# One transformer step on one core: small products of a bidirectional scan joined into longer bursts, the convolution moved ahead of the scan

## The chip, the cores and the metric

One core of one Trainium2 chip runs the whole step. The metric is the device time of one execution in microseconds (us); several runs are taken and their median is given. The engines are TensorE (PE, matrix products), VectorE (DVE), ScalarE (ACT), GpSimd (POOL) and SyncE (SP), which issues all the DMAs here. [...]

## The reference

The step is one trunk layer of width D = 1024 over T = 640 tokens (512 latent, 128 context), in fp32. After a modulated norm, one projection gives r, k, v (512 each), the input of a convolution branch (GLU) and two merge gates. Branch r is a bidirectional RWKV-7 scan over 8 heads of 64:

```python
def step(S, inp):
    rt, wt, kt, vt, at, bt = inp
    sa = jnp.einsum('bhvk,bhk->bhv', S, at)
    S = S * wt[:, :, None, :] + sa[..., None] * bt[:, :, None, :] + vt[..., None] * kt[:, :, None, :]
    return S, jnp.einsum('bhvk,bhk->bhv', S, rt)
```

It is followed by a norm over each head, a bonus term, a gate g and a 512 to 1024 projection. Branch c is GLU, a depthwise convolution of width 31, a norm, swish and a 512 to 1024 projection. The two are merged by sigmoid gates, projected by w_o and added to x; then come the MLP (1024 to 4096, squared ReLU, back to 1024), a residual and a final norm. The final scan states of the context are an output too.

## The kernel before, in words

**Dense products.** Every big fp32 product is split into high and low parts and made of three matmuls (high by high, low by high, high by low) for each of 8 slices of D, 128 x 320 at a time. Weights come by DMA as raw blocks `wr` (256 KB, `splitter`, L240) and are split by ACT (`wh`) and DVE (`wl`). One block of outputs has 48 such matmuls; I call a single one a dense matmul.

**The scan.** The 8 heads go in four pairs p = 0 to 3. For each pair: `prep` makes operands in the tile `ARGH`; `gram` (called by `solve`) makes the Gram products of all 20 chunks of 64 tokens (10 in each direction) in pieces of 32; `inverse` inverts the 64 x 64 triangles, by small DVE operations and three DVE transposes, then by PE products of 32 x 16 and 32 x 32; `build` makes the chunk matrices in five groups of two chunks per direction (matrices `ZB`, `L`, `RB`, `M`, start states `S`); `chain` runs the state through the chunks of a group, a few 64 x 64 products each time and an ACT copy between them; `post` does the norms and gate and writes `out`p to DRAM, from where it is read back into `ath` and split for branch r's projection.

**The order.** A planner at build time (`pick`, `more`, `plan`) keeps these steps as lanes with a rank (`URGENT`) and puts dense matmuls between their bursts; the result is an order written out by hand for PE, DVE and ACT, and each engine goes through its own list in order. The dense blocks come from the list `todo`: k, v, r of each pair, GLU blocks (at place `GLU_AT`), gates, and the side products of branch c (`"c" in ready_sides`) and branch r (`"r" in ready_sides`), which cannot start before their branch is done. Every matmul of these lanes has the line L195 (`mm`), every DVE, ACT and POOL instruction L108, so that pieces are told apart by their tiles.

**The convolution.** `conv_all` waits until the inverse of pair 3 is done and pair 2 is built; five tiles of 128 tokens (`conv_tile`) then run in the buffers `prod`, `Nb`, `Gf`, `Gt` and `E` of the scan, and leave their result split in `ARGH`.

After both branches come w_o, the MLP and the final norm; the change does not touch them.

## Time and profile before

| | us |
|---|---|
| median of 3 runs (lowest, highest) | 1330.57 (1325.54, 1337.10) |
| profiled execution, its own time | 1323.99 |
| its span, first to last instruction | 1322.2 |
| start, up to the first lora2 product | 0 to 56 |
| dense products with the scan's lanes among them | 56 to 677 |
| no dense product on PE | 674 to 729.3 |
| side products, w_o, MLP, end | 729.3 to 1322.2 |

The page's digit rows cut the span into 40 slices of 33 us. A row of a timeline has the start, the length and how many records of the same kind it holds; a matmul's row gives its length in the pipeline, so that the distance of two starts is the cost of one. A small fp32 product leaves two records. What stands in square brackets is how long the engine was idle before, and what ended that.

### The profile page before, as it was taken

How to read it: one execution, taken by the hardware profiler on the slowest of the kernel's cores; microseconds unless marked ns; L12 is line 12 of the kernel's file. 1: busy time of each engine (PE TensorE's matmuls, PEld its weight loads, DVE VectorE, ACT ScalarE, POOL GpSimd, SP SyncE). 2: the span in 40 equal slices, each digit the busy share in tenths (PEclk: the TensorE clock that was granted, in tenths of full speed). 3: DMA queues.
4: the chain of work that ended last, by engine and by line, in shares of the span. 5: the costliest groups of instructions: out<-in, count | busy, mean ns of one | idle time of the engine just before them, and what ended most of it. 6: DMA issues, size and time to landing. Idle time of an engine off the chain costs nothing.

```text
span 1322.2 us, 30685 instructions
## 1 busy us (share of the span) xinstructions
PE 1236.1 (93%) x13110; PEld 1094.7 (83%) x13110; DVE 654.0 (49%) x1342; ACT 505.3 (38%) x1149; POOL 31.4 (2%) x38
## 2 busy tenths in 40 slices
PE   8998899999999999999974899999999999999996
PEld 5776788777777878877741899999999999999996
DVE  5424575376465656245433566654443443443344
ACT  4445346436443643544212223344421331242130
POOL 0000000000000000100100000000000000000000
PEclk8989899999999999999976899989999999999998
DMA  9465433224222311231300683202222222222222
GB/s 371 144 207 171 149 117 122 78 67 150 80 78 81 124 43 58 87 92 54 100 26 8 209 286 122 74 32 78 73 75 81 72 72 81 80 71 74 81 73 80
DMA packets 77785, 136.14 MB, mean 103 GB/s; under 512 B 10768, under 2 KB 27824, under 8 KB 77648
## 3 DMA queue, kind: packets, MB, share of 16 engines
q1 hardware_dynamic: 77648, 134.17, 30.9%
q8 instruction: 103, 1.69, 0.5%
q14 instruction: 34, 0.28, 0.1%
HBM read 112.90 MB, written 21.23 MB: 101 GB/s over the span
## 4 chain that ended last, share of the span: by engine, by line
PE 86%; DVE 4%; ACT 3%; issue 3%; DMA 2%; SPq 0%; POOL 0%; POOLq 0%; DVEq 0%; ACTq 0%
PE ps_mm L195 45%; PE ps_b L195 21%; PE ps_t L195 12%; PE ps_a L195 6%; PE ps_ad L195 2%; DMA z<-tmp 1%; ACT Nb_w L108 1%; DMA par_t<-in_par 1%; DVE E_w L108 1%; DVE Gt_w L108 1%; ACT tmp L108 0%; DVE ARGH_t L108 0%; DMA g<-tmp 0%; DVE Gf_w L108 0%; ACT N_w L108 0%
## 5 line engine op out<-in xcount | busy, mean ns | idle before, releaser
L195 PE MATMUL ps_mm<-xh_t,wh_t 128*128 128x320 f32 x664 | 219.9, 331 | 1.2 <-ACT tmp L108 1.2
L195 PE MATMUL ps_mm<-xl_t,wh_t 128*128 128x320 f32 x664 | 219.8, 331 | 0.0
L195 PE MATMUL ps_mm<-xh_t,wl_t 128*128 128x320 f32 x664 | 217.1, 327 | 0.0
L108 ACT ACTIVATE wh_t<-wr_t 128x512 fp32r<-128x512 f32 x150 | 94.3, 629 | 141.0 <-PE ps_b L195 107.7
L108 DVE TENSOR_TENSOR wl_t<-wr_t,wh_t 128x512 fp32r<-128x512 f32 x150 | 102.8, 686 | 90.6 <-ACT wh_t L108 90.4
L195 PEld LDWEIGHTS ps_mm<-xh_t,wh_t 128*128 128x128 f32 x664 | 128.1, 193 | 19.8 <-issue 14.4
L195 PEld LDWEIGHTS ps_mm<-xl_t,wh_t 128*128 128x128 f32 x664 | 128.2, 193 | 14.6 <-issue 10.8
L195 PEld LDWEIGHTS ps_mm<-xh_t,wl_t 128*128 128x128 f32 x664 | 127.9, 193 | 12.4 <-issue 9.0
L195 PE MATMUL ps_mm<-ARGH_t,wh_t 128*128 128x320 f32 x284 | 77.8, 319 | 11.7 <-ACT wh_t L108 10.9
L108 ACT ACTIVATE tmp<-ps_mm 128x320 f32<-128x320 f32 x80 | 34.9, 436 | 96.7 <-PE ps_mm L195 90.8
L195 PE MATMUL ps_mm<-ARGH_t,wl_t 128*128 128x320 f32 x212 | 67.4, 318 | 0.0
L195 PEld LDWEIGHTS ps_mm<-ARGH_t,wh_t 128*128 128x128 f32 x284 | 53.1, 199 | 12.4 <-ACT wh_t L108 11.1
L108 ACT ACTIVATE mwh<-wr_t 128x512 fp32r<-128x512 f32 x49 | 31.1, 634 | 74.5 <-PE ps_b L195 69.9
L108 DVE TENSOR_TENSOR mwl<-wr_t,mwh 128x512 fp32r<-128x512 f32 x49 | 33.8, 690 | 38.6 <-ACT mwh L108 38.6
L108 DVE TENSOR_TENSOR tmp<-tmp 128x320 f32<-128x320 f32 x64 | 31.2, 489 | 42.7 <-ACT tmp L108 42.7
L108 DVE SCALAR_TENSOR_TENSOR ARGH_t<-ps_mm,mod_t,ARGH_t 128x320 f32<-128x320 f32 (+2 forms) x45 | 22.6, 511 | 59.4 <-PE ps_mm L195 59.4
L195 PE MATMUL ps_mm<-xl,wh_t 128*128 128x320 f32 x140 | 43.9, 314 | 0.0
L195 PE MATMUL ps_b<-ARGH_t,wl_t 128*128 128x320 f32 x140 | 43.2, 308 | 0.0
L195 PE MATMUL ps_b<-xl,wh_t 128*128 128x320 f32 x140 | 43.1, 308 | 0.0
L195 PE MATMUL ps_b<-ARGH_t,wh_t 128*128 128x320 f32 x140 | 42.6, 304 | 0.0
L195 PEld LDWEIGHTS ps_mm<-ARGH_t,wl_t 128*128 128x128 f32 x212 | 41.5, 196 | 0.4 <-DVE wl_t L108 0.4
L108 DVE SCALAR_TENSOR_TENSOR ARGH_t<-ps_b,mod_t,ARGH_t 128x128 f32<-128x128 f32 (+1 forms) x75 | 26.3, 390 | 20.0 <-PE ps_b L195 20.0
(372 smaller groups left out, 3027.6 us busy)
## 6 DMA issues: line engine op xcount, KB each, us to landing
wr_t<-in_w SPq DMA_DIRECT2D x225, 256.0 KB, 2.8
adl_w<-in_adal SPq DMA_DIRECT2D x64, 256.0 KB, 3.3
adar_s<-in_adaw SPq DMA_DIRECT2D x16, 512.0 KB, 8.4
ARGH_t<-in_x SPq DMA_DIRECT2D x8, 640.0 KB, 5.8
z<-tmp SPq DMA_DIRECT2D x32, 160.0 KB, 3.0
gate<-tmp SPq DMA_DIRECT2D x32, 160.0 KB, 1.8
tA_t<-z SPq DMA_DIRECT2D x8, 320.0 KB, 3.4
ath_t<-z SPq DMA_DIRECT2D x8, 320.0 KB, 3.4
```

Source lines behind the costliest of these rows:

```text
L108: return f(*args, **kw)
L195: PE.matmul(out=out, lhsT=lhsT, rhs=rhs, start=start, stop=stop, **kw)
```

## The change

1. Small products of one step are put into one run on PE: Gram products in one run (four before); the 32 x 16 and 32 x 32 products of `inverse` in one run each step (two before); in `build`, the products for the start states, `pb`, `pk` and `pl` in one (three before), with no ACT copy `vr` of reversed v; in `chain`, a state step and the outputs of the same chunk together; the modulation's second product (`ada_late`) for four columns at once.
2. In `inverse` the PE transposes (40 products each pair) go; one DVE transpose of the whole tile comes in (`V.transpose(out=NT, in_=Nd)`).
3. The convolution waits for the GLU blocks alone, which move up in `todo` (`GLU_AT` 12 to 3). It runs in small buffers (`pa`, `pg`, `cy`, `N1`), writes its result to DRAM (`conv0` to `conv3`), and `conv_branch` reads it back and splits it after pair 2 is built.
4. `solve(1)` waits until the convolution has ended (its buffer `N1` is that pair's N), and `post` waits for it too. While the last build runs, raw weights may be held in `ZB` and `L` after it, in place of `vr`.

The diff, cut to its core (`mask_a` and `mask_k` are triangles for both directions, so that no reversed copy is needed):

```diff
-RAWS, SPLITS, SWITCH, EXTRA = ["vr"], ["N1"], 1, 0
+RAWS, SPLITS, SWITCH, EXTRA = ["ZB", "L"], ["N1"], 1, 0
...
-GLU_AT = 12
+GLU_AT = 3
...
-        for i, y0 in enumerate((0, 10)):
-            ps = bank(BANKS[i])[:, 0:320].rearrange("p (y c) -> p y c", c=32)
...
-            A.activation(Gf[:, y0:y0 + 10, :], ps, AF.Copy)
+        near, far = [[bank(b)[:, 0:320].rearrange("p (y c) -> p y c", c=32) for b in bs] for bs in (BANKS, UP_BANKS)]
+        for y in range(NY):
+            for q, rows in enumerate(QUADS):
...
+                mm(near[y // 10][rows, y % 10, :], AB[lo, y, 2 * C + h:2 * C + h + 32], AB[lo, y, h:h + 32], tile_position=(lo.start, rows.start))
+        for y in range(NY):
+            for s in range(2):
+                lo, rows = HEADS[s][0], QUADS[2 * s]
+                mm(far[y // 10][rows, y % 10, :], AB[lo, y, 2 * C:2 * C + 32], AB[lo, y, 32:64], tile_position=(lo.start, rows.start))
+        for i in range(2):
+            A.activation(Gf[:, 10 * i:10 * i + 10, :], near[i], AF.Copy)
             yield "A"
...
+        for i in range(2):
             for s in range(2):
-                A.activation(N[QUADS[2 * s], y0:y0 + 10, 32:64], ps[QUADS[2 * s]], AF.Copy)
+                A.activation(N[QUADS[2 * s], 10 * i:10 * i + 10, 32:64], far[i][QUADS[2 * s]], AF.Copy)
...
-        def products(lhsT, rhs, c0):
-            ps = bank("t")[:, 0:160].rearrange("p (y j) -> p y j", j=16)
-            for c in range(10):
+        def products(lhsT, rhs):
+            ps = bank("t")[:, 0:320].rearrange("p (y j) -> p y j", j=16)
+            for y in range(NY):
                 for q in QUADS:
-                    mm(ps[q, c], lhsT[q, c0 + c, :], rhs[q, c0 + c, 0:16], tile_position=(q.start, q.start))
+                    mm(ps[q, y], lhsT[q, y, :], rhs[q, y, 0:16], tile_position=(q.start, q.start))
             return ps
 
-        for c0 in (0, 10):
-            A.activation(M[:, c0:c0 + 10], products(Gf, Nd, c0), AF.Copy, scale=late)
-            yield
-        for c0 in (0, 10):
-            o = Nd[:, c0:c0 + 10, 0:16]
-            V.tensor_tensor(out=o, in0=products(NT, M, c0), in1=o, op=ALU.add)
-            yield
-
...
+        A.activation(M, products(Gf, Nd), AF.Copy, scale=late)
+        yield
+        o = Nd[:, 0:NY, 0:16]
+        V.tensor_tensor(out=o, in0=products(NT, M), in1=o, op=ALU.add)
+        yield "V"
+
+        V.transpose(out=NT, in_=Nd)
+        Tm = Gf.rearrange("p u t -> p (u t)")[:, 0:NY * 32].rearrange("p (y t) -> p y t", t=32)
+
+        def quads(banks, f):
+
+            ps = [bank(b)[:, 0:320].rearrange("p (y c) -> p y c", c=32) for b in banks]
+            for y in range(NY):
                 for s in range(2):
...
+                    f(ps[y // 10][QUADS[2 * s + 1], y % 10, :], y, *QUADS[2 * s:2 * s + 2])
+            return [(q, slice(10 * i, 10 * i + 10), ps[i][q]) for i in range(2) for q in QUADS[1::2]]
+
+        yield from hold()
+        for q, ys, ps in quads(BANKS, lambda o, y, q0, q1: mm(o, N[q0, y, 32:64], Nd[q0, y, :], tile_position=(q0.start, q1.start))):
+            A.activation(Tm[q, ys], ps, AF.Copy)
         for q in range(4):
             A.activation(N[QUADS[q], :, 32 * (q % 2):32 * (q % 2) + 32], Nd[QUADS[q], 0:NY, :], AF.Copy)
+            if q % 2 == 0:
+                G.memset(N[QUADS[q], :, 32:64], 0.0)
             yield "A"
-        Tm = tmp.rearrange("p i x -> p (i x)")[:, 640:960].rearrange("p (y t) -> p y t", t=32)
-        for y0 in (0, 10):
-            ps = quads(lambda o, y, q0, q1: mm(o, Nd[q1, y0 + y, :], ident[q1, q1], tile_position=(q1.start, q1.start)))
...
+        for q, ys, ps in quads(UP_BANKS, lambda o, y, q0, q1: mm(o, NT[q1, y, :], Tm[q1, y, :], tile_position=(q1.start, q1.start))):
+            A.activation(N[q, ys, 0:32], ps, AF.Copy)
+            yield "A"
+        let_go()
+        yield SEM
...
-        A.activation(vr, rk[2, p][:, ::-1], AF.Copy)
...
-            t = last[0] + SEM
+            yield max(0.0, last[0] + SEM - now[0])
             yield from hold()
             ps = bank(UP_BANKS[1])[:, 0:128 * GC].rearrange("p (y c) -> p y c", c=64)
             for u, (d, c) in enumerate(chunks):
                 for lo, o in HEADS:
-                    tt = C * (c0[d] + c)
-                    mm(ps[o, u, :], (vr if d else rk[2, p])[lo, tt:tt + C], ident[lo, lo])
-            for s, (lo, o) in enumerate(HEADS):
-                A.activation(S[o, s].rearrange("p d c v -> p (d c) v"), ps[o], AF.Copy)
-            yield max(0.0, t - now[0])
+                    tt = C * (NC - 1 - c0[d] - c if d else c0[d] + c)
+                    mm(ps[o, u, :], rk[2, p][lo, tt:tt + C], ident[lo, lo])
 
...
+
+            pl = bank("t").rearrange("p (d c x) -> p d c x", d=2, c=GC)
+            for d, c in chunks:
+                for lo, o in HEADS:
...
             ZB = wt([P, 2, GC, P], "ZB")
             V.tensor_tensor(out=ZB, in0=pb, in1=mask_z.unsqueeze(2).to_broadcast([P, 2, GC, P]), op=ALU.mult)
+            t = last[0] + SEM
             for s, (lo, o) in enumerate(HEADS):
                 A.activation(M[o, s, :, :, 0:64], pk[o, :, :, 0:64], AF.Copy)
+            L = wt([P, 2, GC, P], "L")
+            V.tensor_tensor(out=L, in0=pl, in1=mask_a.unsqueeze(2).to_broadcast([P, 2, GC, P]), op=ALU.mult)
+            for s, (lo, o) in enumerate(HEADS):
                 V.tensor_tensor(out=M[o, s, :, :, 64:128], in0=pk[o, :, :, 64:128],
-                                in1=mask_z[o, :, 64:128].unsqueeze(2).to_broadcast([64, 2, GC, 64]), op=ALU.mult)
-            yield 0.0
-
-            pl = bank("t").rearrange("p (u x) -> p u x", x=P)
...
-            yield 0.0
+                                in1=mask_k[o].unsqueeze(2).to_broadcast([64, 2, GC, 64]), op=ALU.mult)
+                A.activation(S[o, s].rearrange("p d c v -> p (d c) v"), ps[o], AF.Copy)
+            yield max(t - now[0], 0.0)
...
-        while p not in operated or (p and p - 1 not in inverted) or (p > 1 and p - 2 not in built):
+        while p not in operated or len(convolved) < 1 + (p == 1) or (p and p - 1 not in inverted) \
+                or (p > 1 and p - 2 not in built):
             yield 0.3
         yield from gram(p)
         yield from inverse(p)
         inverted.add(p)
+        if p == 3:
+            places.extend(("Gf", "Gt"))
...
-                if (g, i) == (3, GC - 1):
-                    break
+                step = (g, i) != (3, GC - 1)
                 for d in range(2):
                     for s in range(2):
-                        mm(sp[64 * s:64 * s + 64, d, :], M[:, s, d, i, 0:64], S[:, s, d, i, :])
+                        if step:
+                            mm(sp[64 * s:64 * s + 64, d, :], M[:, s, d, i, 0:64], S[:, s, d, i, :])
+                if step and (g, i) != (4, GC - 1):
+                    Sn, n = (S, i + 1) if i < GC - 1 else (SR[(5 * p + g + 1) % RING], 0)
+                    for s in range(2):
+                        lo = slice(64 * s, 64 * s + 64)
+                        A.activation(Sn[lo, s, :, n, :], sp[lo], AF.Copy)
+                elif step:
...
-            for j in range(GC):
+                t = last[0] + SEM
                 for d in range(2):
-                    i = GC - 1 - j if d else j
+                    t0 = C * (GC - 1 - i if d else i)
                     for s in range(2):
-                        mm(po[64 * s:64 * s + 64, 0 if g == 4 else d, C * j:C * j + C], S[:, s, d, i, :], M[:, s, d, i, 64:128],
-                           g < 4 or d == 0, g < 4 or d == 1)
-            for d in range(1 if g == 4 else 2):
+                        mm(po[64 * s:64 * s + 64, d, t0:t0 + C], S[:, s, d, i, :], M[:, s, d, i, 64:128])
+                if i < GC - 1:
+                    yield max(0.0, t - now[0])
...
-        while p and p - 1 not in scanned:
+        while len(convolved) < 2 or (p and p - 1 not in scanned):
...
-        for i in range(4):
-            while i not in gated_linear:
-                yield 1.0
-        while 3 not in inverted:
-            yield 0.5
         ew = wt([P, 2 * P + W], "prod")[0:32]
         DMA.dma_start(out=ew[:, 0:2 * P], in_=I["ce"])
         DMA.dma_start(out=ew[:, 2 * P:], in_=I["cwb"])
-        yield 3.0
+        yield 4.0
...
-        while 2 not in built or 3 not in operated:
-            yield 0.3
-        un = st([P, 2, 4, T], "ARGH", 2, F32R)
-        us, tok = wt([P, 2, 4, P], "prod"), wt([P, 2, W], "Nb")
...
+        convolved.append(0)
+        for i in range(4):
+            while i not in gated_linear:
+                yield 1.0
+        u, ut = [st([P, W], tag) for tag in ("pa", "pg")]
+        pr = wt([P, 2, W], "N1")
         for i in range(5):
-            load(i + 1)
-            yield from conv_tile(i, us[:, i % 2], tok, prods, un)
-        places.extend(("Gf", "Gt"))
-        sides["c"] = Side(un, 8, merge_c, ("kS", "kS"))
-        yield 2.5
-        ready_sides.add("c")
...
+            for j in range(4):
+                DMA.dma_start(out=u[:, P * j:P * j + P], in_=dram(f"glu{j}")[:, P * i:P * i + P])
+            yield 2.5 if i else 4.0
+            yield from conv_tile(i, u, ut, pr)
+        convolved.append(1)
+        spawn(conv_branch(), URGENT["branch"])
+
+    convolved = []
...
+            DMA.dma_start(out=dram(f"conv{j}")[:, P * i:P * i + P], in_=z[:, j])
         yield
-        h, l = (un[:, j, :, P * i:P * i + P] for j in range(2))
-        A.activation(h, z, AF.Copy)
-        yield
-        V.tensor_tensor(out=l, in0=z, in1=h.bitcast(F32), op=ALU.subtract)
-        yield
+
+    def conv_branch():
+
+        while 2 not in built or 3 not in operated:
+            yield 0.3
+        un = st([P, 2, 4, T], "ARGH", 2, F32R)
+        for j in range(4):
+            t = st([P, T], f"ath{j % 2}")
+            DMA.dma_start(out=t, in_=dram(f"conv{j}"))
+            yield 2.5 if j == 0 else 0.5
+            split(un[:, 0, j, :], un[:, 1, j, :], t)
+            yield "V"
+        sides["c"] = Side(un, 8, merge_c, ("kS", "kS"))
+        yield 2.5
+        ready_sides.add("c")
```

**PE, Gram of pair 0.** `ps_mm` rows are dense matmuls; `ps_a` and `ps_b` are the Gram products in two banks. Before:

```order
L195 MATMUL ps_mm<-xh_t,wh_t 128x320
L195 MATMUL ps_a_1468<-ARGH_t 32x32 x40
L195 MATMUL ps_mm<-xl_t,wh_t 128x320
L195 MATMUL ps_b_1512<-ARGH_t 32x32 x40
L195 MATMUL ps_mm<-xh_t,wl_t 128x320
L195 MATMUL ps_a_1555<-ARGH_t 32x32 x20
L195 MATMUL ps_mm<-xh_t,wh_t 128x320
L195 MATMUL ps_mm<-xl_t,wh_t 128x320
L195 MATMUL ps_mm<-xh_t,wl_t 128x320
L195 MATMUL ps_b_1581<-ARGH_t 32x32 x20
L195 MATMUL ps_mm<-xh_t,wh_t 128x320
```

Now:

```order
L196 MATMUL ps_mm<-xh_t,wh_t 128x320
L196 MATMUL ps_a_1396<-ARGH_t 32x32 x40
L196 MATMUL ps_b_1397<-ARGH_t 32x32 x40
L196 MATMUL ps_a_1398<-ARGH_t 32x32 x20
L196 MATMUL ps_b_1399<-ARGH_t 32x32 x20
L196 MATMUL ps_mm<-xl_t,wh_t 128x320
```

The four runs, with one to three dense matmuls between them, are one run. Over the whole order up to the first product of branch r, PE leaves the dense matmuls for a run of other products 313 times before and 182 times now; 131 fewer.

**PE, builds of pair 3.** `ZB_w` rows make RB, `RB_w` rows make M, `M_w,S_w` is the chain's state step, `S_w,M_w` its outputs, `vS_w` begins the next group. Before, the end of one group's first part and what follows:

```order
L195 MATMUL ps_mm<-xh_t,wl_t 128x320
L195 MATMUL ps_mm<-xh_t,wh_t 128x320
L195 MATMUL ps_a_8153<-ZB_w,N_w 64x128 x8
L195 MATMUL ps_mm<-xl_t,wh_t 128x320
L195 MATMUL ps_mm<-xh_t,wl_t 128x320
L195 MATMUL ps_mm<-xh_t,wh_t 128x320
L195 MATMUL ps_mm<-xl_t,wh_t 128x320
L195 MATMUL ps_mm<-xh_t,wl_t 128x320
L195 MATMUL ps_mm<-xh_t,wh_t 128x320
L195 MATMUL ps_a_8171<-RB_w,L_w 128x128
L195 MATMUL ps_b_8172<-RB_w,L_w 128x128
L195 MATMUL ps_a_8171<-RB_w,L_w 128x128
```

Now, group 2 of the same pair up to the beginning of group 3:

```order
L196 MATMUL ps_ad<-S_w,M_w 64x64 x4
L196 MATMUL ps_ad<-M_w,S_w 64x64 x4
L196 MATMUL ps_a_8229<-ZB_w,N_w 64x128 x8
L196 MATMUL ps_a_8240<-RB_w,L_w 128x128
L196 MATMUL ps_b_8241<-RB_w,L_w 128x128
L196 MATMUL ps_a_8240<-RB_w,L_w 128x128
L196 MATMUL ps_b_8241<-RB_w,L_w 128x128
L196 MATMUL ps_a_8240<-RB_w,L_w 128x128
L196 MATMUL ps_b_8241<-RB_w,L_w 128x128
L196 MATMUL ps_a_8240<-RB_w,L_w 128x128
L196 MATMUL ps_b_8241<-RB_w,L_w 128x128
L196 MATMUL ps_ad<-S_w,M_w 64x64 x4
```

Before, dense matmuls stand between the parts of every group of pair 3. Now none stands between group 1's first part and the first product of branch r: all the gates' blocks lie earlier. By the count of dense matmuls from the first lora2 product on, the Gram products of pair 3 come after 1119 of them before and after 1721 now; the first product of branch r after 1728 before and after 1824 now, the 96 more being blocks of branch c. The five convolution tiles lie between dense matmuls 536 and 1050 now; before, the last two lie after the last of the 1728. Now the five build groups of pair 1 stand after dense matmuls 1368, 1416, 1464, 1560 and 1608 as runs of 42 to 48 rows with no dense matmul inside; before, no run between 1204 and 1641 is longer than 17 rows.

**SP, the end of the scan.** `out_ns` is the final state of the last pair, `gate` rows are results of gate blocks, `glu` rows are the convolution's loads, `pg_t` rows are the loads of `post`. Before:

```order
L1037 DMA out_ns<-ade_t 256x1x64
L1128 DMA prod_w<-glu_3537 128x128
L1128 DMA prod_w<-glu_4881 128x128
L613 DMA gate_8271<-tmp 128x320
L240 DMA vr_w<-in_w 128x512
L613 DMA gate_8271<-tmp 128x320
L240 DMA wr_t<-in_w 128x512
L1067 DMA pg_t<-g_1230 128x640
L613 DMA gate_8389<-tmp 128x320
L1085 DMA out_8412<-Y_w 128x640
L613 DMA gate_8389<-tmp 128x320
```

Now:

```order
L1211 DMA mc_8003<-rS_w 128x320
L1237 DMA kS_w<-gate_4690 128x640
L1211 DMA mc_8114<-rS_w 128x320 x2
L1237 DMA kS_w<-gate_4855 128x640
L241 DMA ZB_w<-in_w 128x512
L241 DMA L_w<-in_w 128x512
L1034 DMA out_ns<-ade_t 256x1x64
L1058 DMA pg_t<-g_1247 128x640
L1076 DMA out_8625<-Y_w 128x640
L1195 DMA ath_t<-out_7728 128x640
L1195 DMA ath_t<-out_8625 128x640
```

After the last state, only the load of g, the write of `out3` and the reloads of the two last `out` tiles stand in the queue; the gates' writes and the convolution's loads come earlier.

## Rows read from the trace of the kernel before

**Rows 1.** Page: busy tenths in 40 slices, and the granted clock in tenths.

```profile
PE   8998899999999999999974899999999999999996
...
PEclk8989899999999999999976899989999999999998
```

**Rows 2.** Windows: stretch, length, engines' busy us (instructions), clock, DMA share, GB/s.

```profile
677.00:729.30 52.30, 23.84 (x56) 10.52 (x56) 18.00 (x33) 10.50 (x20) 1.09 (x2) 0.57 0.05 16
729.30:1322.20 592.90, 576.26 (x3888) 572.99 (x3888) 282.48 (x570) 184.64 (x360) 3.41 (x4) 0.98 0.29 95
```

**Rows 3.** Windows of 20 us in the hole.

```profile
680.00:700.00 20.00, 10.06 (x24) 4.02 (x23) 6.60 (x13) 2.69 (x6) 0.54 (x1) 0.50 0.00 0
700.00:720.00 20.00, 11.57 (x26) 4.86 (x24) 5.46 (x11) 2.48 (x5) 0.54 (x1) 0.67 0.00 0
```

**Rows 4.** Timeline of PE: a burst among dense matmuls (a convolution tile's products).

```profile
659.22 0.30 PE L195 MATMUL ps_mm<-xh_t,wh_t 128*128 128x320 f32 x1
659.46 1.12 PE L195 MATMUL ps_t<-Nb_w,cf_w 64*128 64x512 f32 x2
660.51 0.41 PE L195 MATMUL ps_mm<-xl_t,wh_t 128*128 128x320 f32 x1
660.76 0.31 PE L195 MATMUL ps_mm<-xh_t,wl_t 128*128 128x320 f32 x1
```

**Rows 5.** Chain of waits: start, us, a run of dense matmuls.

```profile
789.45 3.52 PE ps_mm L195 x24
```

**Rows 6.** Timeline of PE: the hole, its ends and two of its waits.

```profile
673.75 0.31 PE L195 MATMUL ps_mm<-xh_t,N_w 128*128 128x320 f32 x1
677.05 1.43 PE L195 MATMUL ps_t<-cst_t,prod_w 128*128 128x128 f32 x8 [2.99 <-DVE E_w L108]
...
699.03 2.08 PE L195 MATMUL ps_t<-cst_t,prod_w 128*128 128x128 f32 x8 [3.87 <-DVE E_w L108]
...
729.30 0.90 PE L195 MATMUL ps_mm<-ARGH_t,wh_t 128*128 128x320 f32 x2 [10.92 <-ACT wh_t L108]
```

**Rows 7.** Timeline of PE: within the Gram products of pair 3.

```profile
465.88 0.62 PE L195 MATMUL ps_a<-ARGH_t 64*32 64x32 f32 x22 [1.45 <-issue]
```

**Rows 8.** Windows: Gram to build of pair 0, Gram of pair 2 to pair 3's, Gram to build of pair 3.

```profile
142.38:213.42 71.04, 65.38 (x1218) 55.36 (x1217) 42.10 (x92) 33.45 (x76) 3.42 (x5) 0.93 0.39 124
355.12:461.61 106.49, 98.92 (x1786) 81.79 (x1786) 61.11 (x130) 49.46 (x122) 5.73 (x6) 0.97 0.29 92
461.61:555.95 94.34, 90.67 (x1704) 75.18 (x1704) 47.53 (x109) 40.90 (x105) 3.70 (x5) 0.98 0.19 61
```

**Rows 9.** Timeline of PE and of DVE: a PE transpose and a DVE transpose in the inverse.

```profile
538.84 0.82 PE L195 MATMUL ps_t<-cst_t,Gt_w 32*32 32x32 f32 x40
...
177.76 2.05 DVE L108 STREAM_TRANSPOSE prod_w<-Nb_w 128x1024 f32<-128x1024 f32 x1
```

**Rows 10.** Timeline of PE: one build group of pair 3, the first row of each part.

```profile
618.13 0.32 PE L195 MATMUL ps_a<-M_w,ARGH_t 64*64 64x128 f32 x1
...
619.95 0.34 PE L195 MATMUL ps_t<-cst_t,ARGH_t 64*64 64x64 f32 x4
...
621.57 1.09 PE L195 MATMUL ps_a<-ZB_w,N_w 64*64 64x128 f32 x16
...
623.66 0.37 PE L195 MATMUL ps_a<-RB_w,L_w 64*128 64x128 f32 x1
```

**Rows 11.** Timeline of ACT and of DVE: the same group's RB copy and last additions.

```profile
622.76 0.60 ACT L108 ACTIVATE RB_w<-ps_a 128x512 f32<-128x512 f32 x1 [1.26 <-PE ps_a L195]
...
625.46 0.68 DVE L108 TENSOR_TENSOR M_w<-ps_b,M_w 128x512 f32<-128x512 f32 x1
```

**Rows 12.** Timeline of PE, then SP: post of pair 3, its write, the reload.

```profile
632.92 0.76 PE L195 MATMUL ps_t<-Y_w,cst_t 128*64 128x320 f32 x4
...
652.68 0.32 SPq L1085 DMA_DIRECT2D out<-Y_w  x1
...
725.10 1.05 SPq L1202 DMA_DIRECT2D ath_t<-out  x2
```

More of the change, by code (lines that the diff above doesn't have):

```diff
@@ L615, in gate, with ada_late @@
         yield from dense(xh_, xl_, evac)
-    def ada_late(col):
+    def ada_late(col, e):
         raws = []
@@ L736, in operands @@
             yield "V"
-            V.tensor_tensor(out=AB[:, ys, 3 * C:4 * C], in0=tv(at), in1=cs, op=ALU.mult)
+            V.tensor_tensor(out=AB[:, ys, 4 * C - 1:3 * C - 1:-1] if d else AB[:, ys, 3 * C:4 * C], in0=tv(at), in1=cs, op=ALU.mult)
             yield "V"
@@ L753, in first @@
         return GC * ((g + d) % 5)
-    vr = wt([P, T], "vr")
     def bonus(p):
@@ L979, in build @@
             A.activation(RB, pf, AF.Copy)
-            yield max(t, last[0] + SEM) - now[0]
+            yield
             pu = [bank(b) for b in BANKS]
@@ L1151, in conv_tile @@
             mm(ps, cf[lo, 0:P], ut[lo])
[L1152 to L1153 removed]
+            V.scalar_tensor_tensor(out=pr[:, 0], in0=ps, scalar=cf[:, P + 384:P + 385], in1=cg[:, 0], op0=ALU.add, op1=ALU.mult)
+            V.tensor_tensor(out=pr[:, 1], in0=ps, in1=cg[:, 1], op=ALU.mult)
             yield
[L1155 to L1165 removed]
+            ps = bank("t")
+            at, n = (lo, 64) if i < 4 else (slice(0, P), P)
+            for j in range(2):
+                o = P + 192 * j + 64 - (0 if i < 4 else 64 * r)
+                mm(ps[at], cf[:, o:o + n], pr[:, j], j == 0, j == 1)
+            if i == 4 and r:
+                V.tensor_tensor(out=y, in0=ps, in1=y, op=ALU.add)
+            else:
+                A.activation(y[at], ps[at], AF.Copy)
+            yield
         s6, mv, r1 = st([P, 6], "cs6"), st([P, 2], "cmv"), st([P, 1], "cr1")
@@ L1170, in conv_tile @@
         yield 2.5
+        yn = u
         V.tensor_scalar(out=yn, in0=y, scalar1=mv[:, 0:1], scalar2=r1, op0=ALU.subtract, op1=ALU.mult)
@@ L1265, in ada_all @@
     def ada_all():
+        e = wt([P, 4, P], "ade")
         for c in range(16, 48):
-            yield from ada_late(c)
+            yield from ada_late(c, e)
     def fill():
@@ L1581, in _pack @@
     s, t = np.arange(64)[:, None], np.arange(64)[None, :]
-    c[:, CST_MA:CST_MA + P] = 1.0
-    for h in range(2):
-        o = 64 - 64 * h
-        c[64 * h:64 * h + 64, CST_MA + o:CST_MA + o + 64] = s > t
-    c[:, CST_MZ:CST_MZ + 256] = 1.0
+    c[:, CST_MA:CST_MA + 256] = c[:, CST_MZ:CST_MZ + 256] = 1.0
     for d in range(2):
+        for h in range(2):
+            o = CST_MA + 128 * d + 64 - 64 * h
+            c[64 * h:64 * h + 64, o:o + 64] = s > (63 - t if d else t)
         c[:, CST_MZ + 128 * d + 64:CST_MZ + 128 * d + 128] = np.tile(s <= (63 - t if d else t), (2, 1))
+        c[:, CST_MK + 64 * d:CST_MK + 64 * d + 64] = np.tile(s >= t if d else s <= t, (2, 1))
     for g in range(4):
```

103 lines of the change are left out of this document (23 added, 80 removed).

## The prediction, as put on record before the result

> **What bounds the kernel now.** I read the page's digit rows first: PE is busy nine tenths or more nearly everywhere, and the one broad dent, with a low granted clock beside it, lies a little past the middle [rows 1]. The windows then split the span. From 729.3 us to the end PE is busy 576.3 of 592.9 us; the change does not touch that part, so it can only shift it [rows 2]. In the dent, 677 to 729.3, PE works 23.84 us at a mean clock of 0.57 [rows 2], in its middle at 0.50 and 0.67 [rows 3]: two convolution tiles run there with no dense matmul between, and each PE product waits for a DVE or ACT step; the start of one tile is 22 us before that of the next (677.05 to 699.03) [rows 6]. So three stretches matter: dense matmuls with lanes among them (56 to 677), the hole, and the rest. In the first, time is PE's: a dense matmul costs 0.147 us (24 in 3.52 us) [rows 5], and whatever else PE does is added to it.
>
> **What the order now changes.** The hole's convolution goes early, among dense matmuls. But pair 1's Gram products wait for the whole convolution (1061 dense matmuls are done by then, 573 before), and pair 3's come after 1721 instead of 1119. So the dense matmuls run out before the scan does: pair 3's inverse has some left, its build groups 1 to 4, chain and post have none. I cost it up to the first product of branch r, which stands at 729.3 before [rows 6], in two legs: up to pair 3's Gram, and from there.
>
> **Leg 1, up to pair 3's Gram.** From that Gram at 461.6 [rows 8] to the hole at 677 the old kernel takes 215.4 us, of which 609 dense matmuls are 89.4 us; the other 126 us are lane work and its waits. Of these, three convolution tiles with their first products are about 20. A build group, with chain, is about 7 us of PE (0.69, 1.1 for pb and pk, 1.2 for pl, 1.09, 1.15 [rows 10], and as much as a quarter more for the chain's other step and the start states), and the four of pair 2 that come ahead of pair 3's Gram now are about 30. So some 75 us of what is done by 677 now still lies ahead when pair 3's Gram starts. From 677:
> - minus 75, as said;
> - plus 12, two more convolution tiles among dense matmuls (23.84 us at about half clock, so half of that at full clock) [rows 2];
> - minus 15 for joined runs. Around a run, the dense matmuls' starts are 0.24 and 0.25 us apart and not 0.147 [rows 4], so a run costs about 0.2 us beside its own products. 131 runs fewer in all; about 76 lie in this leg. The other end is 0.42 us: a dense matmul is 0.30 us long in the pipeline, 0.41 after a run, and if nothing of either is hidden the loss is 0.15 and 0.26. I take 0.2, which is what the starts show;
> - minus 5 for PE transposes: two runs of 0.82 us for each of three pairs [rows 9]. The DVE transpose that comes in is 2.05 us [rows 9]; it lengthens the inverse, not PE's work, and DVE is far from full;
> - nothing for the Gram itself. It has an idle time of 1.45 us inside, ended by "issue" [rows 7]: PE had no instruction. The same number of products comes in one run now, so I keep it; between 2 us gained and 2 us lost for each pair;
> - plus 14 for pair 1's five build groups, which now stand bare, 48 dense matmuls apart. Inside one, PE must wait for the RB copy (0.60) and for two additions on DVE, of which the last starts 1.8 us after the products begin and takes 0.68 [rows 10, 11], and for a state copy: about 2.8 us in each, hidden under dense matmuls before. Ends: 8 and 27.
>
> 677 − 75 + 12 − 15 − 5 + 14 = 608 for the start of pair 3's Gram.
>
> **Leg 2, pair 3's Gram to the first product of branch r.**
> - Gram to build: 60. The shortest before is pair 0's, 71.0 us; pair 3's took 94.3, with dense matmuls between [rows 8]. Fewer steps and little filling now, but pair 2's last group, its chain and its post are in the way. Ends 48 and 71.
> - Build group 0, with dense matmuls: 9.5. Groups 1 to 4, bare: the parts in turn (2.7 us of first products, 1.1, the RB copy, 1.15, the additions, the chain's steps) come to 8.5 us at full clock, and to about 13 if PE's 5 us take twice as long [rows 10, 11]. I take 10.5, the middle: the hole's rows, the nearest bare stretch, show 0.50 and 0.67 [rows 3], but PE idled half of it, more than here. 42 for the four.
> - End of the chain 5; post from its first product to the write of `out3`, 19.8 before (632.92 to 652.68) [rows 12], 19 now that nothing is between; the write's landing, the reload and the split 7.5 (reload to first product alone 4.2: 725.10 to 729.30 [rows 6, 12]).
>
> 60 + 9.5 + 42 + 5 + 19 + 7.5 = 143; ends 118 and 168. So the first product of branch r comes at 751, 21.7 us later than before.
>
> **The rest** is shorter by the 96 dense matmuls of branch c that are done by then, 14.1 us.
>
> **Costed at nothing:** the convolution's writes, reads and the wider constants (SP queues 328 transfers for 317 and the DMA engines stand at 0.29 of their time or below in these stretches [rows 2]; with that cover gone a late reload would delay branch c, which has pair 3's build to wait in); the wait of `post` for the convolution (it ends well ahead of pair 0's post by the order, and only ACT's and DVE's post steps would queue behind it); the missing `vr` copy, since ACT is no bound.
>
> **Sum.** 21.7 − 14.1 = +7.6 us against the profiled execution's 1323.99, so 1331.6. The runs' median is 1330.57, 0.5% above that execution; with the same step it gives 1338 us. About 1% (13 us) is what a measurement of this kernel tells from no change, so this is within it.
>
> **Rivals.**
> - *Bare groups keep the full clock.* PE's 5 us of 8.5 in a bare group is a higher share than the hole's 23.84 of 52.3 [rows 2]; against it, the products are small. Groups 8.5 instead of 10.5 and 5 us less in the inverse and post: −13, 1325 us. Chance 0.17.
> - *A run costs all of its filling and draining*, 0.42 us instead of 0.2: 131 × 0.22 = −29, 1309 us, faster. For it: several runs are products of quarter-array size, whose switch I read only at a convolution tile; against it, the starts [rows 4]. Chance 0.20.
> - *The clock falls in every stretch without dense matmuls*, the bare groups of pair 1 among them. [...] Groups of pair 3 at 13 (+10) and of pair 1 about 2.6 us longer each (+13): +23, 1361 us, slower. For it: 0.50 in the hole at once when the dense matmuls ended [rows 3]. Chance 0.23.
> - That the change does not do what it says is excluded for the joined runs: the order has them.
>
> [...]
>
> **Numbers.** Forecast 0.40, the rivals 0.17, 0.20 and 0.23. The forecast's own range, by the uncertain lumps and the inverse, is 1324 to 1352. The 8-in-10 range runs from just under the second rival to a little over the third: 1306 to 1368. Faster by over 1%: the second rival and 0.05 of the first, 0.25. Slower by over 1%: the third and 0.15 of the forecast, 0.38. Within 1%: 0.37.
>
> **What would show it.** Right: pair 3's Gram near 608; PE free of dense matmuls for about 80 us before the first product of branch r, which comes near 751; the rest of the span some 14 us shorter; around each remaining run the starts still 0.24 us apart. Wrong: Gram of pair 3 before 595 (the runs cost more than I took), a bare group of 8.5 us at clock 1.00, or of 13 us at 0.5; a Gram-to-build stretch of under 48 us; a weight block late after the bare stretch.

## The result, and the profile after

The change made the kernel slower: a median of 1381.51 us (1380.17 to 1386.65, 4 runs) against 1328.17 (1325.54 to 1337.1) for the kernel before on the same chip, ratio 1.0396 with a 95% interval of 1.0338 to 1.0455. The forecast was 1338 and its range ended at 1368. The profiled execution took 1380.17 us, its span is 1377.8.

Two corrections to what stands above. Rows name the `rhs` of `mm` first, so `S_w,M_w` is the chain's state step and `M_w,S_w` its outputs, not the other way round. And the product at 729.3 us before [rows 6] is not the first of branch r but the first of branch c: the first eight results after it go to `rS_w`, which is branch c's. Branch r's first product comes 96 dense matmuls later, in the kernel before at

```profile
746.63 0.45 PE L195 MATMUL ps_mm<-ARGH_t,Gf_w 128*128 128x320 f32 x2
```

In the kernel after, branch c's 96 are done earlier, so the prediction's sum, which takes them off the rest, still compares like with like.

Page of the kernel after: busy tenths and granted clock of the 40 slices, against [rows 1]. Clocks are shares of full speed; the lowest that a window here shows is 0.50 [rows 3], and "half clock" stands for that.

```profile
PE   8999899988998988998667669999999999999997
...
PEclk9889999998999999899769679999999999999998
```

The dent has not gone. It is shallower and wider: five slices with a 6 or a 7 (34.4 us each) where before there were two at 7 and 4. The windows of the kernel after are cut at the prediction's own marks: up to pair 3's Gram, from there to the first product of branch r, and the rest. Columns are those of [rows 2].

```profile
56.00:655.69 599.69, 533.24 (x6889) 442.63 (x6887) 290.42 (x587) 237.52 (x564) 20.09 (x17) 0.93 0.33 104
655.69:803.38 147.69, 94.27 (x1768) 78.44 (x1764) 64.37 (x139) 43.99 (x112) 5.82 (x4) 0.72 0.22 68
803.38:1377.80 574.42, 559.89 (x3792) 556.79 (x3792) 275.96 (x557) 181.52 (x355) 3.40 (x4) 0.99 0.27 90
```

The same view of the kernel before, from 56 us to the mark from which the prediction counted:

```profile
56.00:677.00 621.00, 584.82 (x8824) 474.42 (x8824) 323.31 (x670) 282.94 (x706) 25.53 (x27) 0.97 0.32 103
```

In the first leg PE works 51.6 us less than before up to 677, but it is idle 66.5 us instead of 36.2, and the mean clock is 0.93 instead of 0.97. The rows at the two marks, from PE's timeline:

```profile
655.69 0.86 PE L196 MATMUL ps_a<-ARGH_t 64*32 64x32 f32 x78
...
660.98 0.28 PE L196 MATMUL ps_b<-ARGH_t 64*32 64x32 f32 x6 [2.52 <-issue]
...
803.38 0.90 PE L196 MATMUL ps_mm<-ARGH_t,wh_t 128*128 128x320 f32 x2 [11.92 <-ACT wh_t L108]
```

The second answers [rows 7], the third the last of [rows 6]. Set beside the prediction's terms:

| | forecast | after | miss |
|---|---|---|---|
| pair 3's Gram starts | 608 | 655.7 | +47.7 |
| Gram to first product of branch r | 143 | 147.7 | +4.7 |
| from there to the end | 592.9 − 14.1 = 578.8 | 574.4 | −4.4 |

The sum, 48.0 us, is all of 1377.8 − (1322.2 + 7.6). The miss lies in leg 1. The view of PE's waits says what is new (what waited, on whom; us in total, times, longest), 56 to 800 us, first before, then after:

```profile
PE ps_ad L195 <- ACT ade_t L108: 1.6, 4, 0.4
PE ps_ad L195 <- DVE M_w L108: 1.2, 2, 0.9
```

```profile
PE ps_ad L196 <- ACT S_w L108: 26.4, 32, 2.8
...
PE ps_ad L196 <- DVE M_w L108: 5.4, 10, 1.2
...
PE ps_ad L196 <- ACT ade_t L108: 1.5, 4, 0.4
...
PE ps_ad L196 <- ACT Y_w L108: 1.0, 1, 1.0
```

`ps_ad` is the chain's bank (what `bank` hands out in the kernel: a tile of 512 columns that PE writes its results to). A wait of its products for ACT's state copy did not exist before; now there are 32. PE's timeline of one bare group of pair 3 after shows where it sits:

```profile
741.79 0.33 PE L196 MATMUL ps_ad<-S_w,M_w 128*64 128x64 f32 x2 [0.71 <-DVE M_w L108]
742.39 0.45 PE L196 MATMUL ps_ad<-S_w,M_w 128*64 128x64 f32 x6 [0.27 <-DVE M_w L108]
743.48 0.45 PE L196 MATMUL ps_ad<-M_w,S_w 128*64 128x64 f32 x8 [0.64 <-ACT S_w L108]
...
747.54 0.66 PE L196 MATMUL ps_ad<-S_w,M_w 128*64 128x64 f32 x8
748.87 0.45 PE L196 MATMUL ps_ad<-M_w,S_w 128*64 128x64 f32 x8 [0.67 <-ACT S_w L108]
749.25 1.09 PE L196 MATMUL ps_a<-ZB_w,N_w 64*64 64x128 f32 x16
```

And the copies on ACT that end those two waits:

```profile
742.87 0.56 ACT L108 ACTIVATE S_w<-ps_ad 64x128 f32<-64x128 f32 x2 [2.02 <-PE ps_ad L196]
...
748.25 0.57 ACT L108 ACTIVATE S_w<-ps_ad 64x128 f32<-64x128 f32 x2 [0.57 <-PE ps_ad L196]
```

In `chain` the state step of a chunk writes the bank's first quarter, ACT copies it from there into the next chunk's state, and the chunk's outputs, which read the old state and write other columns of the same bank, come right behind. The second copy writes another buffer of the ring than the one the outputs read, and they wait all the same; so what they share with the copy is the bank. Before, the outputs of a whole group came later in a burst of their own, when the copies were long done; only where the last state is copied out did they follow closely, and there the wait could be seen (PE's timeline before):

```profile
521.52 0.45 PE L195 MATMUL ps_ad<-S_w,M_w 128*64 128x64 f32 x8
522.35 0.69 PE L195 MATMUL ps_ad<-M_w,S_w 128*64 128x64 f32 x16 [0.38 <-ACT ade_t L108]
```

Those outputs read nothing of `ade_t`. In all these rows the outputs go to the partitions and the bank that the copy reads, and start 0.05 us after its end: 743.48 after 743.43, 748.87 after 748.82, and before 522.35 after 522.30 (the copy into `ade_t` starts at 522.02 and takes 0.28). Whether the wait hangs on the program's tile or on something of the memory behind it, no run parts. PE ran its rows in the order of its list, so while the outputs wait, everything behind them does, dense matmuls included: at 202.87 us they start after a wait of 0.65, and the dense matmul behind them starts at 203.25. In these 26.4 us PE ran nothing.

### The profile page after: what moved, and what is told of

Its sections match the earlier page's. It is cut to its first block, busy times and chain, and to the rows that moved or that the text cites. A ratio compares the mean times of both kernels' runs of the same rounds, so it can differ in the third digit from the quotient of the medians.

```text
span 1377.8 us, 30059 instructions
## 1 busy us (share of the span) xinstructions
PE 1238.7 (90%) x12790; PEld 1113.6 (81%) x12790; DVE 661.7 (48%) x1354; ACT 491.1 (36%) x1096; POOL 30.7 (2%) x30
## 4 chain that ended last, share of the span: by engine, by line
PE 65%; DVE 5%; ACT 4%; issue 3%; DMA 1%; POOL 0%; POOLq 0%; DVEq 0%; ACTq 0%; SPq 0%
PE ps_mm L196 33%; PE ps_b L196 20%; PE ps_t L196 7%; PE ps_a L196 3%; PE ps_ad L196 1%; ACT S_w L108 1%; DVE Y_w L108 1%; ACT pg_t L108 1%; DVE N_w L108 0%; DVE kk_t L108 0%; DMA out<-Y_w 0%; DVE M_w L108 0%; DVE cy_w L108 0%; DVE wl_t L108 0%; DVE Gt_w L108 0%
## 5 line engine op out<-in xcount | busy, mean ns | idle before, releaser
L196 PE MATMUL ps_mm<-xh_t,wh_t 128*128 128x320 f32 x680 | 226.2, 333 | 0.0
L196 PE MATMUL ps_mm<-xh_t,wl_t 128*128 128x320 f32 x680 | 224.6, 330 | 1.0 <-DVE wl_t L108 1.0
L196 PE MATMUL ps_mm<-xl_t,wh_t 128*128 128x320 f32 x680 | 223.9, 329 | 0.5 <-issue 0.5
L196 PEld LDWEIGHTS ps_mm<-xh_t,wh_t 128*128 128x128 f32 x680 | 135.5, 199 | 16.4 <-issue 12.3
L196 PEld LDWEIGHTS ps_mm<-xh_t,wl_t 128*128 128x128 f32 x680 | 135.7, 200 | 14.0 <-issue 11.3
L196 PEld LDWEIGHTS ps_mm<-xl_t,wh_t 128*128 128x128 f32 x680 | 135.3, 199 | 12.3 <-issue 10.9
L196 PE MATMUL ps_mm<-ARGH_t,wh_t 128*128 128x320 f32 x300 | 82.8, 324 | 12.6 <-ACT wh_t L108 11.9
L196 PEld LDWEIGHTS ps_mm<-ARGH_t,wh_t 128*128 128x128 f32 x300 | 56.3, 200 | 13.7 <-ACT wh_t L108 12.3
L108 DVE TENSOR_TENSOR ZB_w<-ps_a,cst_t 128x512 f32<-128x512 f32 x20 | 13.8, 690 | 86.4 <-PE ps_b L196 86.4
L196 PE MATMUL ps_ad<-M_w,S_w 128*64 128x64 f32 x320 | 19.7, 250 | 27.9 <-ACT S_w L108 26.4
```

Source lines behind the costliest of these rows:

```text
L108: return f(*args, **kw)
L196: PE.matmul(out=out, lhsT=lhsT, rhs=rhs, start=start, stop=stop, **kw)
```

## The experiments

Ratios are against the kernel before on the same chip, with the 95% interval.

**Each half alone.** First the joined runs with the convolution where it was before, then the early convolution, with its waits, in the kernel before.

```
# e1: the change, without the early convolution
-GLU_AT = 3
+GLU_AT = 12
-        while p not in operated or len(convolved) < 1 + (p == 1) or (p and p - 1 not in inverted) \
-                or (p > 1 and p - 2 not in built):
+        while p not in operated or (p and p - 1 not in inverted) or (p > 1 and p - 2 not in built):
...
```

> The changed kernel with the convolution put back where it stood before (late, in the scan's buffers, no wait of pair 1 or of the post steps for it, GLU blocks at place 12); the joined products and the DVE transpose stay. Theory A: the loss comes from the early convolution, which makes pair 1 late, lets the dense matmuls run out and leaves build groups bare at a low clock; the joined runs by themselves save about 0.18 us for each of some 100 runs saved. Then this is 1303 to 1318 us, and the hole at the end of the convolution stays. Theory B: the joined runs themselves hurt, since chain and DVE waits lie bare in them; then this is 1350 to 1380 us.

1355.56 us, 1.0209 (1.0160 to 1.0259). Joining alone, whose runs I had priced as a saving, costs about 2%. The wait is there without the early convolution (PE's waits of this kernel):

```profile
PE ps_ad L196 <- ACT S_w L108: 23.1, 32, 2.8
```

```
# e2: the kernel before, with the early convolution
-GLU_AT = 12
+GLU_AT = 4
+        while p not in operated or len(convolved) < 1 + (p == 1) or (p and p - 1 not in inverted) \
+                or (p > 1 and p - 2 not in built):
...
+        u, ut = [st([P, W], tag) for tag in ("pa", "pg")]
...
+        spawn(conv_branch(), URGENT["branch"])
```

> The kernel before with only the early convolution (small buffers, result in DRAM, waits of pair 1 and post; GLU blocks at place 4, one later than in the change), small products in short runs as before. Theory A: 1385 to 1405 us, slower than the whole change because the saving of the joined runs is missing; the Gram products of pair 3 start near 660 us and the first product of branch r near 800. Theory B: 1325 to 1340 us.

1360.97 us, 1.0253 (1.0196 to 1.0310): between the two ranges. The halves cost 27 and 33 us, together 60, and the change 53. Neither theory of a single culprit stands.

**Is it the clock?** One dummy dense product is added wherever the planner would leave PE idle: in the change some 380, in the kernel before 280.

```
+            elif not merged and mm_ends and mm_ends[0] <= now[0]:
+                mm_ends.popleft()
+                mm(bank()[:, 0:H2], xh[:, 0, 0:P], xh[:, 0, 0:H2])
+                mm_ends.append(last[0])
```

> The changed kernel with about 380 extra matmuls (128 x 320, high part only, their result is not used) on PE wherever the planner has neither a lane's step nor a dense matmul ready. They do nothing but keep PE at work. Theory A with the clock as the larger part: of the 125 us that PE's work took at half clock up to the first product of branch r some 80 come back to full clock, and the time falls by 25 to 40 us, to 1340 to 1357. Theory A with latency as the larger part (ACT and DVE steps between the products of a bare group set the pace): 1370 to 1385 us, with the clock at 1.00 in the stretch and the same length.

1397.74 us, 1.0532 (1.0477 to 1.0586), outside both ranges: the mean clock rose from 0.934 to 0.970 and the kernel became 16 us longer.

> The kernel before with about 280 such extra matmuls, nearly all in the hole of the last two convolution tiles. If the clock matters there: PE's 24 us of work at a clock of 0.57 become about 12 and the hole is 8 to 12 us shorter, 1318 to 1322 us. If only the ACT and DVE steps set it: 1325 to 1333 us.

1349.35 us, 1.0155 (1.0104 to 1.0206), again outside both; the mean clock of the profiled execution is 0.973, before 0.959. In both, the dummies cost more than the higher clock gave. That is all they show: a higher clock bought in this way does not repair the change, and what the clock itself costs stays open by them.

**The wait, taken away.** The chunk's outputs are issued ahead of its state step, so that they stand in front of the copy.

```
                 for d in range(2):
+                    t0 = C * (GC - 1 - i if d else i)
+                    for s in range(2):
+                        mm(po[64 * s:64 * s + 64, d, t0:t0 + C], S[:, s, d, i, :], M[:, s, d, i, 64:128])
+                for d in range(2):
                     for s in range(2):
                         if step:
                             mm(sp[64 * s:64 * s + 64, d, :], M[:, s, d, i, 0:64], S[:, s, d, i, :])
...
-                        mm(po[64 * s:64 * s + 64, d, t0:t0 + C], S[:, s, d, i, :], M[:, s, d, i, 64:128])
```

> The changed kernel with the chain's output products of a chunk put ahead of its state step and not behind it (they do not need the state step's result). Theory C1: in the change the outputs stand right behind the state step, in the same bank and beside the state copies, and PE waits at each for the ACT copy of the state; 34 us of PE's idle time are there against 2.8 before. Then most of that idle time goes and the time is 1345 to 1362 us. Rival: the wait is a true one and only moves to the next chunk's products: 1374 to 1386 us.

1314.30 us, 0.9904 (0.9869 to 0.9939): 67 us less than the change, well below the expected range, and less than before. The waits of this kernel:

```profile
PE ps_ad L196 <- DVE M_w L108: 4.9, 10, 0.8
...
PE ps_ad L196 <- ACT S_w L108: 0.6, 1, 0.6
```

The bare group of pair 3 in its timeline: outputs, then the state step, and nothing waits for ACT.

```profile
692.69 0.33 PE L196 MATMUL ps_ad<-M_w,S_w 128*64 128x64 f32 x2 [0.71 <-DVE M_w L108]
693.29 0.39 PE L196 MATMUL ps_ad<-M_w,S_w 128*64 128x64 f32 x5 [0.27 <-DVE M_w L108]
...
693.52 0.45 PE L196 MATMUL ps_ad<-S_w,M_w 128*64 128x64 f32 x7
...
696.24 0.45 PE L196 MATMUL ps_ad<-M_w,S_w 128*64 128x64 f32 x8
696.53 0.40 PE L196 MATMUL ps_ad<-S_w,M_w 128*64 128x64 f32 x8
696.86 1.09 PE L196 MATMUL ps_a<-ZB_w,N_w 64*64 64x128 f32 x16
```

But moving two lines also moves what the planner does elsewhere, since it decides by the times that it adds up. So the two were parted: e9 has the change's order in every other row and only these products exchanged (the planner is still told of them in the old places); e10 has e5's order in every other row and the outputs behind the state step again.

```
+    def mm(out, lhsT, rhs, start=True, stop=True, emit=True, count=True, **kw):
+        if emit:
+            PE.matmul(out=out, lhsT=lhsT, rhs=rhs, start=start, stop=stop, **kw)
+        if not count:
+            return
# e9: outputs issued first (count=False), costed in the old place (emit=False); e10 the reverse
```

> The changed kernel with the outputs put ahead of the state step on PE, but counted by the planner where they stood, so that every other row of PE, DVE and ACT stays in the change's order (e5 changed the planner's order too). Theory W: the waits for the state copy are the larger part of e5's 67 us: chain's idle time falls from 34 to under 10 us, half-clock time falls with it, 1332 to 1350 us. Theory O: the planner's other order (pair 3's Gram after 1672 dense matmuls for 1745, no bare build groups of pair 1) is the larger part: 1352 to 1372 us.

1345.76 us, 1.0147 (1.0108 to 1.0186).

> The counterpart of e9: e5's order in every other row, with the outputs put back behind the state step on PE. Theory W: the waits return, 1345 to 1365 us, most of the way from e5's 1314 to the change's 1381. Theory O: 1318 to 1335 us.

1355.71 us, 1.0217 (1.0183 to 1.0250). The waits for the state copy in e9, then in e10:

```profile
PE ps_ad L197 <- ACT S_w L108: 4.6, 4, 2.6
```

```profile
PE ps_ad L197 <- ACT S_w L108: 21.3, 32, 0.9
```

By the ratios the wait is worth 33 us in the change's order (1.0396 − 1.0147) and 42 in e5's (1.0217 − 0.9904), the planner's other order 24 to 32. **The wait alone is over half of the 53 us.** Of its 33 us in the change's order, 21.8 are idle time of PE (26.4 − 4.6). The others come with it and were not parted from it: in e9 the bare groups of pair 3 run at full clock, as its window over them shows (columns as in [rows 2]; the kernel after has 0.87 there, see below).

```profile
711.70:745.00 33.30, 25.72 (x586) 22.45 (x586) 18.61 (x40) 16.44 (x52) 0.00 (x0) 1.00 0.11 33
```

Why the other order is better was not tried by itself.

**What the other knobs do.** Pair 3's Gram sooner, by a higher rank of `solve` in e1 (1 to 0.75); no wait of pair 1 for the whole convolution in the change (its halves computed in its own input buffer); the convolution ahead in the kernel before (rank 1.6 to 0.7).

```
# e6, on e1            -solve=1    +solve=0.75
# e7, on the change
-        while p not in operated or len(convolved) < 1 + (p == 1) or (p and p - 1 not in inverted) \
+        while p not in operated or len(convolved) < 1 or (p and p - 1 not in inverted) \
# e8, on the kernel before   -conv=1.6   +conv=0.7
```

> As e1_joined_only (joined runs, convolution late), with one number changed: the rank of the Gram and inverse lane, 0.75 for 1, so that it comes ahead of the next build group when both want the banks. By the order pair 3's Gram then comes after 1274 dense matmuls and not 1356 (1143 before), and two convolution tiles are left bare and not three. Theory C2: what is left to do when the dense matmuls run out sets the time; a bare tile is 22 us where one among dense matmuls is 6: 1330 to 1342 us. Rival: the tail does not matter, the loss lies in the joined runs: 1350 to 1362 us.

1342.03 us, 1.0108 (1.0061 to 1.0155), 13.5 less than e1; pair 3's Gram is at 513 us instead of 528.

> The changed kernel with the convolution's products made in two halves of 256 columns, in the buffer of its input, so that pair 1's Gram need not wait for its end (the convolution has about 20 more short runs, some 5 us). Pair 1's Gram then comes after 834 dense matmuls and not 1085, pair 3's after 1611 and not 1745; the same four build groups of pair 3 are bare. Theory C2 with the wait of pair 1 as the cause: pair 3's inverse gets dense matmuls beside it again, 1335 to 1355 us. Rival: the four bare groups and the waits inside are the loss, the late Gram is not: 1372 to 1390 us.

1366.09 us, 1.0276 (1.0198 to 1.0354), between the two ranges. Pair 1's Gram goes from 426.8 to 347.8 us, but pair 3's only from 655.7 to 642.2, and 15 us are won. Moving one pair's start is not moving the last one's end.

> The kernel before with one number changed: the rank of the convolution's lane, 0.7 for 1.6, so that its steps go ahead of the build's when both are ready. By the order one convolution tile is then left bare when the dense matmuls run out, and not two. Theory C2: a bare tile is 22 us, one among dense matmuls 6: 16 us less, 1308 to 1318 us. Rival: the hole is given back elsewhere: 1324 to 1334 us.

1318.14 us, 0.9926 (0.9886 to 0.9965): the hole of [rows 6] can be made smaller with no early convolution at all.

**Versions meant to beat both.** e11 is e5 with the convolution's rank at 0.95. e12 keeps the joined runs of inverse, build and chain, outputs first, but the Gram products in four runs and the convolution late, with ranks of 0.75 (`solve`) and 0.95 (`conv`).

```
# e11, on e5:   conv=0.95
# e12, on the change: e5's outputs first, e1's late convolution, and
+solve=0.75, conv=0.95
+        for i, y0 in enumerate((0, 10)):
+            ps = bank(BANKS[i])[:, 0:320].rearrange("p (y c) -> p y c", c=32)
...
+            A.activation(Gf[:, y0:y0 + 10, :], ps, AF.Copy)
             yield "A"
```

> e5 (the change with the outputs first) with the rank of the convolution's lane 0.95 for 1.6. By the order pair 3's Gram then comes after 1511 dense matmuls for 1672, and about two build groups of pair 3 stand bare for four. Theory C2 (what is left when the dense matmuls run out): two groups of 7.9 us less what they cost among dense matmuls, 10 to 20 us: 1294 to 1306 us. If the tail does not matter: 1310 to 1318.

1334.87 us, 1.0051 (1.0024 to 1.0078): a miss. Pair 3's Gram came 23 us earlier than in e5 (586.5), but its inverse's products 9 us later (655.3 for 646.7), with the last of pair 2's build and its post standing between. A Gram's place is not a finish.

> The other way to join both lessons: joined runs in inverse, build and chain, outputs first, the Gram products in four runs as before, the convolution late as before, with ranks of 0.75 for the Gram lane and 0.95 for the convolution's. By the order one convolution tile is left bare (two before). Theory C2: 16 us less for the tile and about 0.18 us for each of some 90 runs saved: 1288 to 1302 us. If only the one or the other holds: 1306 to 1316.

**1283.77 us, 0.9672 (0.9634 to 0.9710): faster than both kernels**, and below the expected range. No wait of `ps_ad` products is left among its waits. One convolution tile stands bare instead of two, as PE's timeline shows, and the side products begin 35.9 us earlier than in [rows 6]:

```profile
662.76 2.08 PE L196 MATMUL ps_t<-cst_t,prod_w 128*128 128x128 f32 x8 [3.87 <-DVE E_w L108]
...
681.35 1.13 PE L196 MATMUL ps_t<-cst_t,Nb_w 128*128 128x128 f32 x8 [3.18 <-DVE Nb_w L108]
...
693.40 0.90 PE L196 MATMUL ps_mm<-ARGH_t,wh_t 128*128 128x320 f32 x2 [10.92 <-ACT wh_t L108]
```

## Why the prediction was wrong

**The step that failed** is the pricing of the joined chain: "minus 15 for joined runs", with the wait for "a state copy" charged only to the five bare groups of pair 1, inside "plus 14". The order showed the outputs right behind the state step, and `chain` shows both in one bank; I read the joining as fewer runs and never asked what the second half waits for. It waits for ACT at nearly every chunk, under dense matmuls too, since these stand behind it in PE's queue. Of its 26.4 us, 20.2 lie in leg 1. With the wait gone and everything else in its place (e9), the kernel takes 1345.76 us, inside the range I gave; but that is partly luck, for leg 1 is still 30 us too long there, and leg 2 and the rest 13 and 5 too short. The [0.38 <-ACT ade_t] of the kernel before was the hint, and I passed over it.

**Leg 1, +47.7.** In e9 pair 3's Gram starts at 637.9 us, so 17.8 of the miss are the wait. The other 30, which I worked out by adding up PE's records of e9 and of the kernel before by kind, work and idle time before it, are these:
- The convolution, +15. Its three tiles before the hole took 21.9 us there (3.0 of it idle time at the hole's edge); all five take 48.9 in e9, so 27 more and not 12. "Half of that at full clock" was the error. In e9 8.4 us of it are PE's waits, and some 7 come from one group of products in the first four tiles: before, a tile's two halves stand in one run, and their products start in pairs; in the early form each half is a run of its own, and each takes as long as the two together did. PE's timeline before, then after (e9 has the same row):

```profile
594.19 0.64 PE L195 MATMUL ps_t<-Gf_w,cf_w 128*64 128x512 f32 x1
594.20 0.64 PE L195 MATMUL ps_t<-Gt_w,cf_w 128*64 128x512 f32 x1
594.67 0.59 PE L195 MATMUL ps_t<-Gf_w,cf_w 128*64 128x512 f32 x1
...
596.06 0.42 PE L195 MATMUL ps_mm<-xh_t,wh_t 128*128 128x320 f32 x1
```

```profile
296.34 1.93 PE L196 MATMUL ps_t<-N_w,cf_w 128*64 128x512 f32 x4
298.20 0.42 PE L196 MATMUL ps_mm<-xl_t,wh_t 128*128 128x320 f32 x1
```

  Eight records took 1.87 us before, four take 1.86 after, and there are two such runs in a tile.
- The work carried over, with the bare groups and the transposes, +9: the lanes' products and waits fall by 57 us, where −75 − 5 + 14 said 66.
- The `ada` products, which I left out, +6.
- The dense matmuls, with what stands around each run, +1: 14 less, as forecast (15), but by errors that cancel. The trace has 290 stretches of dense matmuls in this leg before and 151 after, so some 140 runs fewer and not 76. Outside the half-clock stretches a run cost 0.19 us, as I took it (0.2). Some 25 us saved, then, of which about 11 went back: the time that dense matmuls spend at half clock rose from 21 to 45 us.

The line between the second and the last of these is not sharp: the 75 came from a sum that holds the cost of the runs carried over, and some of the 140 runs are those.

**Leg 2, right by cancellation.** 147.7 against 143, but 130.4 in e9 and 131.7 in e5: I had put it 12 us too long, and the waits, with the lower clock beside them (0.72 over this leg, 0.85 in e5), filled that up again. The bare groups are 11.2 to 11.4 us apart after (their `ZB_w,N_w` rows start at 738.00, 749.25, 760.61 and 771.80) where I took 10.5, and 8.0 apart in e5 (688.90, 696.86, 704.81). So the 10.5 was near by luck: of the 3.3 us by which a group is longer after than in e5, 1.3 are its two waits for the state copy (0.64 and 0.67). Windows of 33 us over them, first of the kernel after, then of e5:

```profile
733.90:766.90 33.00, 23.54 (x438) 20.15 (x434) 13.55 (x28) 13.29 (x43) 0.00 (x0) 0.87 0.05 14
```

```profile
685.00:718.00 33.00, 25.40 (x584) 22.10 (x582) 18.39 (x39) 16.19 (x52) 0.00 (x0) 1.00 0.07 21
```

In e5, PE is busy 25.40 us of 33 with 584 records (two a product) and the clock is 1.00. After, it does three quarters as many in the same time, and the clock is 0.87.

**The rest, −4.4.** Shorter by 18.5 us than [rows 2] has it, where I said 14.1. The direction and the reason (branch c's blocks already done) held; the size did not, since those 96 matmuls took 17.3 us before (729.30 to 746.63; clock 0.50 up to 735, 0.81 over the whole), and not 14.1.

**The rivals.** *Bare groups keep the full clock* holds in e5: 8.0 us and 1.00, where that rival said 8.5. It was hidden by the wait. *A run costs all of its filling and draining*: no, 0.19 us. *The clock falls in every stretch without dense matmuls* named the sign, with 1361 still 20 us short, but not the mechanism: it wanted groups of 13 us, and in e5 the bare groups run at full clock. Two other stretches without dense matmuls in e5, pair 3's inverse and its post up to branch r's first product, do not:

```profile
640.00:657.80 17.80, 7.69 (x404) 7.01 (x403) 12.24 (x21) 2.41 (x5) 0.00 (x0) 0.57 0.29 89
...
719.00:741.35 22.35, 5.17 (x38) 3.26 (x34) 6.99 (x12) 4.45 (x9) 1.95 (x1) 0.62 0.21 62
```

There PE is idle more than half of the time. So four stretches without dense matmuls, with PE busy for 0.77, 0.71, 0.43 and 0.23 of them, had clocks of 1.00, 0.87, 0.57 and 0.62: that such a stretch is a slow one does not hold for the first, e5's bare groups. What sets the clock, no run shows.

**What joining is worth.** In leg 1 of the change it gave back some 25 us of PE's time, as far as the runs can be counted to it, and it cost 33 to 42 by one wait. Once the wait is gone the saving stands: with the early convolution in both, e5 (joined, outputs first) is at 0.9904 and e2 (not joined) at 1.0253, 46 us apart, the planner's order included. e12's 44 us below the kernel before are not joining's alone, since two ranks differ as well, and a rank by itself gave 10 us in e8.

**The early convolution** costs 33 us by itself (e2). Its tiles fill no hole where they now stand, among dense matmuls, and they delay pair 3's scan: in e2 its Gram starts at 615.6 us instead of 461.6, and PE has no dense matmul from 644.3 to 681.3 and from 704.0 to 780.3 us, 113 us against 55 before. How the 33 us divide between this and the longer tiles was not measured.

**Open.** What a second bank for the outputs would give, without the exchange, was not tried. Nor is it known why the order that the planner makes in e5 is 24 to 32 us better than the change's.

## What to carry to other kernels

When two bursts of small products are joined, look for a copy on another engine between them that reads the bank they share: what was hidden while other work stood between them became here a wait of all that stood behind it in PE's list, 26.4 us. Put the products that need nothing of that copy in front of the ones that feed it; here two lines exchanged were worth 33 to 42 us. And work that is moved to where the bound engine has plenty to do fills nothing (the early convolution cost 33 us by itself): count what that engine will have left beside the last dependent chain. When moved work is cut into more runs, look whether products that started in pairs still do: here eight records in pairs took 1.87 us, and four without a pair 1.86.

## What the runs showed of the hardware that was not expected

- Products into one part of `ps_ad` waited for ACT's read of another part: 0.64 to 0.90 us each in the bare groups of pair 3, where the copy takes 0.56, and up to 2.8 us where ACT's copy was itself late (2.79 at 547.01: the copy ran from 546.40 to 546.95, behind one into `N_w`).
- Small products alone held the full clock in e5's bare groups: 584 records (292 products) in 33 us, PE busy 25.40 us, clock 1.00. In the same kernel's bare inverse, 404 records in 17.8 us, PE busy 7.69 us, it was 0.57.
- Products of the convolution that start in pairs, into the two 64-partition halves of a bank, took 1.87 us for eight records; four records of one half alone took 1.86 (594.19 to 596.06 before, 296.34 to 298.20 after).
- The idle time ended by "issue" inside the Gram products did not grow with the longer runs: 1.89, 1.60, 1.65 and 1.45 us in the four pairs before, none, 1.27, 1.75 and 2.52 after. That the prediction put nothing for it held. "Issue" is time in which PE waited for nothing that the profile shows; that it had no instruction then, as the prediction says, was my reading.
